# A softmax over 32768 columns: stores moved from GpSimd's queue to ScalarE's, loads pinned six tiles ahead

## The chip, the cores and the metric

One NeuronCore of a Trainium2 chip. The metric is the device time of one execution in microseconds (us), taken over several executions; a profile is taken of one such execution. On the profile's page an engine's busy share is the part of the span in which it works. A run is called slow when it is over 1.5% above the fastest run of the same kernel; ratios use the fast runs alone, while the times in us are medians of all runs. A ratio below is the mean time of one kernel's fast runs over that of the kernel before in the same rounds, on the same chip, so it is not quite the ratio of the medians quoted beside it.

## The reference

```python
def setup_inputs():
    batch, seq, vocab = 16, 256, 32768
    return {"logits": randn(batch, seq, vocab) as float32, "temperature": 1.0}

def reference(logits, temperature):
    scaled = logits / temperature
    scaled = scaled - scaled.max(axis=-1, keepdims=True)
    exp_scaled = np.exp(scaled)
    return exp_scaled / exp_scaled.sum(axis=-1, keepdims=True)
```

That is 537 MB in and 537 MB out, each touched once. Nothing is multiplied as a matrix; what matters is moving the bytes.

## The kernel before

Each row of 32768 columns is cut into four, so that a tile is 128 partitions x 8192 columns of float32 (4 MB), and there are 128 tiles. Six tile buffers fill the memory that is used on the core. A tile is worked in two chunks of 4096 columns. A tile has a first half (maxima on VectorE, exponentials with running sums on ScalarE, the minimum chain that joins the four quarter rows, and `ee`, a tiny exponential of 128x2) and a second half (the sum, its reciprocal, the factor `f`, two scalings, the store).

```python
for t in range(n_tiles):
    ...
    xs = xpool.tile([P, IC], fp32, tag="x", name="xs")          # one of six buffers
    nc.sync.dma_start(out=xs[:rp, :dn], in_=x[r0:r1, d0 : d0 + dn])
    for g0, gn in chop(dn, CC):                                 # two chunks
        nc.vector.tensor_reduce(out=nm[...], in_=xc, axis=X, op=A.max, negate=True)
        nc.scalar.activation(out=xc, in_=xc, func=Exp, bias=nm[...], accum_out=ssum[...])
    with tc.high_priority():
        nc.vector.tensor_reduce(out=nMh[...], in_=nm[:rp], axis=X, op=A.min)
        ...                                                     # shuffles and minima
        nc.scalar.activation(out=ee[:rp], in_=nm[:rp], func=Exp, bias=nM[:rp], scale=-1.0)
        nc.vector.tensor_tensor_reduce(out=ttj, in0=ee, in1=ssum, ...)   # the sum
        ...                                                     # shuffles, reciprocal
        nc.scalar.activation(out=f[:rp], in_=ee[:rp], func=Copy, scale=rS[:rp])
    ...
            nc.vector.tensor_scalar_mul(out=xc, in0=xc, scalar1=f[...])  # chunk 1
            nc.scalar.activation(out=xc, in_=xc, func=Copy, scale=f[...])  # chunk 0
    nc.gpsimd.dma_start(out=o[r0:r1, d0 : d0 + dn], in_=xs[:rp, :dn])
```

The source is not the issue order. A scheduler orders the instructions of each engine when the program is built, and the traces of this case show each engine working through its list in order: in the changed kernel ScalarE stands idle for 10.37 us before `ee` of tile 68 (1547.44 in the timeline further down), though the exponential that stands after it in the list (1547.82, the second chunk of tile 65) has had its maximum since 1471. So the built order has to be read from the built program or the trace.

Of the kernel before, what the change touches and what calls it, by code (L numbers as in the profile page):

```python
# [1 line left out]

# [4 lines left out]


_SPLIT = 4  # L10
_IC = 8192
_CC = 4096
_SBUF_KB = 192
_SCALE_ON_DVE = {1, 4, 7}


@with_exitstack
def kernel(
    ctx: ExitStack,
    tc: tile.TileContext,  # L20
    logits: bass.AP,
    temperature: bass.AP,
    out: bass.AP,
):
    nc = tc.nc

    inv_t = 1.0 / float(temperature)

    P = nc.NUM_PARTITIONS
    xf = logits.flatten_outer_dims()  # L30
    of = out.flatten_outer_dims()
    N, V = xf.shape

    SPLIT = _SPLIT
    while SPLIT > 1 and (V % SPLIT or (N * SPLIT) % P or V // SPLIT < 512):
        SPLIT //= 2
    x = xf.rearrange("n (h v) -> (n h) v", h=SPLIT) if SPLIT > 1 else xf
    o = of.rearrange("n (h v) -> (n h) v", h=SPLIT) if SPLIT > 1 else of
    NR, VR = x.shape
    n_tiles = (NR + P - 1) // P  # L40

    IC = min(_IC, VR)
    CC = min(_CC, IC)

    def chop(total: int, step: int) -> list[tuple[int, int]]:
        return [(s, min(step, total - s)) for s in range(0, total, step)]

    dchunks = chop(VR, IC)
    NDC = len(dchunks)
    NCH = len(chop(VR, CC))  # L50
    XBUFS = max(NDC + 2, (_SBUF_KB * 1024) // (IC * 4))

    xpool = ctx.enter_context(tc.tile_pool(name="x", bufs=XBUFS))
    spool = ctx.enter_context(tc.tile_pool(name="stats", bufs=8))

    fp32 = mybir.dt.float32
    Exp = mybir.ActivationFunctionType.Exp
    Copy = mybir.ActivationFunctionType.Copy
    X = mybir.AxisListType.X
    A = mybir.AluOpType  # L60
    n_rounds = SPLIT.bit_length() - 1

    for t in range(n_tiles):
        r0 = t * P
        r1 = min(r0 + P, NR)
        rp = r1 - r0

        nm = spool.tile([P, NCH], fp32, tag="nm", name="nm")
        ssum = spool.tile([P, NCH], fp32, tag="ssum", name="ssum")
        ee = spool.tile([P, NCH], fp32, tag="ee", name="ee")  # L70
        f = spool.tile([P, NCH], fp32, tag="f", name="f")
        ttj = spool.tile([P, NCH], fp32, tag="ttj", name="ttj")
        nMh = spool.tile([P, 1 + n_rounds], fp32, tag="nMh", name="nMh")
        Sh = spool.tile([P, 1 + n_rounds], fp32, tag="Sh", name="Sh")
        rS = spool.tile([P, 1], fp32, tag="rS", name="rS")

        slots = []
        c = 0
        for d0, dn in dchunks:
            xs = xpool.tile([P, IC], fp32, tag="x", name="xs")  # L80
            slots.append(xs)
            nc.sync.dma_start(out=xs[:rp, :dn], in_=x[r0:r1, d0 : d0 + dn])  # L82
            for g0, gn in chop(dn, CC):
                xc = xs[:rp, g0 : g0 + gn]
                nc.vector.tensor_reduce(  # L85
                    out=nm[:rp, c : c + 1], in_=xc, axis=X, op=A.max, negate=True
                )
                if inv_t != 1.0:
                    nc.vector.tensor_scalar_mul(
                        out=nm[:rp, c : c + 1], in0=nm[:rp, c : c + 1], scalar1=inv_t  # L90
                    )
                nc.scalar.activation(  # L92
                    out=xc,
                    in_=xc,
                    func=Exp,
                    bias=nm[:rp, c : c + 1],
                    scale=inv_t,
                    accum_out=ssum[:rp, c : c + 1],
                )
                c += 1  # L100

        with tc.high_priority():
            nc.vector.tensor_reduce(out=nMh[:rp, 0:1], in_=nm[:rp], axis=X, op=A.min)  # L103
            for j in range(n_rounds):
                mask = [i ^ (1 << j) for i in range(32)]
                nc.vector.stream_shuffle(  # L106
                    out=nMh[:rp, j + 1 : j + 2], in_=nMh[:rp, j : j + 1], mask=mask
                )
                nc.vector.tensor_tensor(  # L109
                    out=nMh[:rp, j + 1 : j + 2],  # L110
                    in0=nMh[:rp, j : j + 1],
                    in1=nMh[:rp, j + 1 : j + 2],
                    op=A.min,
                )
            nM = nMh[:, n_rounds : n_rounds + 1]
            nc.scalar.activation(  # L116
                out=ee[:rp], in_=nm[:rp], func=Exp, bias=nM[:rp], scale=-1.0
            )
            nc.vector.tensor_tensor_reduce(  # L119
                out=ttj[:rp],  # L120
                in0=ee[:rp],
                in1=ssum[:rp],
                scale=1.0,
                scalar=0.0,
                op0=A.mult,
                op1=A.add,
                accum_out=Sh[:rp, 0:1],
            )
            for j in range(n_rounds):
                mask = [i ^ (1 << j) for i in range(32)]  # L130
                nc.vector.stream_shuffle(  # L131
                    out=Sh[:rp, j + 1 : j + 2], in_=Sh[:rp, j : j + 1], mask=mask
                )
                nc.vector.tensor_tensor(  # L134
                    out=Sh[:rp, j + 1 : j + 2],
                    in0=Sh[:rp, j : j + 1],
                    in1=Sh[:rp, j + 1 : j + 2],
                    op=A.add,
                )
            nc.vector.reciprocal(out=rS[:rp], in_=Sh[:rp, n_rounds : n_rounds + 1])  # L140
            nc.scalar.activation(out=f[:rp], in_=ee[:rp], func=Copy, scale=rS[:rp])  # L141

        c = 0
        for i, (d0, dn) in enumerate(dchunks):
            xs = slots[i]
            for g0, gn in chop(dn, CC):
                xc = xs[:rp, g0 : g0 + gn]
                if (c % 8) in _SCALE_ON_DVE:
                    nc.vector.tensor_scalar_mul(  # L149
                        out=xc, in0=xc, scalar1=f[:rp, c : c + 1]  # L150
                    )
                else:
                    nc.scalar.activation(  # L153
                        out=xc, in_=xc, func=Copy, scale=f[:rp, c : c + 1]
                    )
                c += 1
            nc.gpsimd.dma_start(out=o[r0:r1, d0 : d0 + dn], in_=xs[:rp, :dn])  # L157


# [1 line left out]
_INS = ['logits', 'temperature']  # L161
_OUTS = [((16, 256, 32768), 'float32')]
#: Inputs that are plain numbers.
_NUMBERS = {'temperature': 1.0}


# [26 lines left out]
```

## Time and profile before

| | before |
|---|---|
| time, median of 4 runs | 2549.78 us (2544.84 to 2555.9) |
| span of the profiled run | 2541.2 us |
| DMA share, rate | 99.6% of 16 engines, 423 GB/s |
| VectorE, ScalarE busy | 61%, 59% |

From the page of the kernel before: the span, the busy times, the rows of 40 equal slices (each digit is the busy share in tenths, then GB/s), the DMA queues with packets, MB and share of the 16 engines, and the first line of the chain that ended last.

```profile
span 2541.2 us, 4377 instructions
...
DMA  9999999999999999999999999999999999999997
GB/s 413 431 430 429 424 428 429 426 427 425 424 427 424 429 424 422 424 427 422 423 425 419 429 424 426 424 425 426 423 428 424 426 425 427 426 424 423 425 426 327
...
q1 hardware_dynamic: 18432, 536.88, 50.6%
q0 software_dynamic: 18432, 536.88, 49.0%
...
DMA 87%; issue 6%; DVE 5%; another core or an unknown queue 0%; ACT 0%; POOL 0%; POOLq 0%; SPq 0%
```

The DMA row is at 9 in 39 of 40 slices, and loads (q1) and stores (q0) together take 99.6% of the engines. VectorE and ScalarE are idle for about two fifths of the time. In the trace's packet records the usual 32 KB packet takes 1213 ns on both queues; 32,768 such packets on 16 engines make 2484 us, which is the floor of the DMA work as measured here.

The longest waits of the kernel before, in total, in number, and the longest one:

```profile
POOL out_dram L157 <- DVE Sh L131: 2345.5, 122, 20.1
...
DVE nm L85 <- DMA xs<-in_logits_dram: 961.8, 125, 13.1
```

VectorE waits for data that DMA has not brought yet, and GpSimd's wait for VectorE is a store waiting for its tile: both go back to DMA. The queue that issues the loads (SPq, SyncE's) waits in turn for stores to land, once for each of the 122 loads after the first six, because a landed store is what frees a buffer:

```profile
SPq L82 <- DMA out_dram<-xs: 2400.7, 122, 61.0
```

The DMA issues, with the median time from issue to landing:

```profile
xs<-in_logits_dram SPq DMA_DIRECT2D x128, 4096.0 KB, 36.9
out_dram<-xs POOLq DMA_DIRECT2D x128, 4096.0 KB, 34.7
```

A transfer of 4 MB takes 37 us because about two loads and two stores share the engines (36.9 and 34.7 us at one of each per 19.8 us are 1.9 and 1.8 in flight). The first load, which is alone at the head of its queue, takes 12.3 us (issued at 0.74, landed at 13.08).

### The profile page before, as it was taken

The page shows a single profiled execution, that of the slowest core. Times are in us where ns is not written, and L with a number is a line of the kernel's source. Part 1 is how long each engine was busy: PE and PEld are TensorE (multiplying, and loading weights), DVE is VectorE, ACT ScalarE, POOL GpSimd, SP SyncE. Part 2 cuts the span into 40 slices and gives each one's busy share as a digit, 9 for nine tenths or more (in the row PEclk, how much of TensorE's full clock was granted, in tenths as well). Part 3 has the DMA queues.
Part 4 walks back from the last instruction along what each step waited for, and adds up shares of the span by engine and source line. Part 5 has one row for each costly group of instructions (what it writes and reads, how often), then busy time and mean ns, then how long its engine had stood idle before and what let it go on. Part 6 is the DMA issues. An engine that isn't in the chain of part 4 may idle for free.

```text
span 2541.2 us, 4377 instructions
## 1 busy us (share of the span) xinstructions
DVE 1548.3 (61%) x2432; ACT 1496.3 (59%) x897; POOL 70.2 (3%) x132
## 2 busy tenths in 40 slices
DVE  7665566665566655666556665666556665666554
ACT  6556655556656565565655566555665656555664
POOL 0000000000000000000000000000000000000000
DMA  9999999999999999999999999999999999999997
GB/s 413 431 430 429 424 428 429 426 427 425 424 427 424 429 424 422 424 427 422 423 425 419 429 424 426 424 425 426 423 428 424 426 425 427 426 424 423 425 426 327
DMA packets 36898, 1074.04 MB, mean 423 GB/s; under 512 B 4096, under 2 KB 4096, under 8 KB 4096
## 3 DMA queue, kind: packets, MB, share of 16 engines
q1 hardware_dynamic: 18432, 536.88, 50.6%
q0 software_dynamic: 18432, 536.88, 49.0%
q14 instruction: 34, 0.28, 0.0%
HBM read 536.87 MB, written 536.87 MB: 423 GB/s over the span
## 4 chain that ended last, share of the span: by engine, by line
DMA 87%; issue 6%; DVE 5%; another core or an unknown queue 0%; ACT 0%; POOL 0%; POOLq 0%; SPq 0%
DMA xs<-in_logits_dram 45%; DMA out_dram<-xs 43%; DVE xs L149 3%; DVE nm L85 2%; DVE ttj L119 0%; ACT xs L92 0%; POOL out_dram L157 0%; SPq L82 0%; POOLq L157 0%; DVE nMh L106 0%; DVE nMh L109 0%; DVE Sh L131 0%; POOLq L188 0%; DVE Sh L134 0%
## 5 line engine op out<-in xcount | busy, mean ns | idle before, releaser
L85 DVE TENSOR_REDUCE nm<-xs 128x1 f32<-128x4096 f32 x256 | 1130.1, 4415 | 961.8 <-DMA xs<-in_logits_dram 961.8
L92 ACT ACTIVATE xs<-xs,nm 128x4096 f32<-128x4096 f32 x256 | 949.2, 3708 | 1006.4 <-DVE nm L85 1006.4
L153 ACT ACTIVATE xs<-xs,f 128x4096 f32<-128x4096 f32 x128 | 474.5, 3707 | 4.2
L149 DVE TENSOR_SCALAR xs<-xs,f 128x4096 f32<-128x4096 f32 x128 | 300.7, 2350 | 0.8 <-ACT f L141 0.8
L157 POOL DMA_DIRECT2D out_dram<-xs x128 | 70.0, 547 | 2450.4 <-DVE Sh L131 2345.5
L92 ACT ACTIVATION_READ_ACCUMULATOR xs<-xs,nm 128x1 f32 x256 | 47.7, 186 | 0.0
L109 DVE TENSOR_TENSOR nMh<-nMh 128x1 f32<-128x1 f32 x256 | 40.9, 160 | 4.4
L134 DVE TENSOR_TENSOR Sh<-Sh 128x1 f32<-128x1 f32 x256 | 39.9, 156 | 0.0
L131 DVE STREAM_SHUFFLE Sh<-Sh 128x1 f32<-128x1 f32 x256 | 38.8, 152 | 0.0
L106 DVE STREAM_SHUFFLE nMh<-nMh 128x1 f32<-128x1 f32 x256 | 38.8, 152 | 0.0
L116 ACT ACTIVATE ee<-nm,nMh 128x2 f32<-128x2 f32 x128 | 35.8, 280 | 0.0
L141 ACT ACTIVATE f<-ee,rS 128x2 f32<-128x2 f32 x128 | 35.8, 280 | 0.0
L119 DVE CUSTOM_DVE_ANT_0 ttj<-ee,ssum 128x2 f32<-128x2 f32 x128 | 19.3, 151 | 3.1 <-ACT ee L116 3.1
L140 DVE RECIPROCAL rS<-Sh 128x1 f32<-128x1 f32 x128 | 21.0, 164 | 0.0
L103 DVE TENSOR_REDUCE nMh<-nm 128x1 f32<-128x2 f32 x128 | 19.8, 155 | 0.0
L119 DVE DVE_READ_ACCUMULATOR2_ANT Sh<- 128x1 f32 x128 | 10.6, 83 | 0.0
L92 ACT ACT_TABLE_LOAD x1 | 1.3, 1283 | 13.2 <-DMA xs<-in_logits_dram 13.2
L131 DVE LOAD_MASK_SELECT Sh<-Sh x256 | 3.6, 14 | 0.1
L106 DVE LOAD_MASK_SELECT nMh<-nMh x256 | 3.6, 14 | 0.1
L174 POOL MEMSET const-float32-0.0<- 128x1 f32 x1 | 0.1, 98 | 0.2 <-issue 0.2
L174 POOL MEMSET const-bfloat16-1.0<- 128x1 bf16 x1 | 0.1, 101 | 0.0
L174 POOL MEMSET const-float32-1.0<- 128x1 f32 x1 | 0.1, 98 | 0.0
(1 smaller groups left out, 0.1 us busy)
## 6 DMA issues: line engine op xcount, KB each, us to landing
xs<-in_logits_dram SPq DMA_DIRECT2D x128, 4096.0 KB, 36.9
out_dram<-xs POOLq DMA_DIRECT2D x128, 4096.0 KB, 34.7
```

What stands on the lines that cost most here:

```text
L85: nc.vector.tensor_reduce(out=nm[:rp, c : c + 1], in_=xc, axis=X, op=A.max, negate=True)
L92: nc.scalar.activation(out=xc, in_=xc, func=Exp, bias=nm[:rp, c : c + 1], scale=inv_t, accum_out=ssum[:rp, c : c + 1],)
L106: nc.vector.stream_shuffle(out=nMh[:rp, j + 1 : j + 2], in_=nMh[:rp, j : j + 1], mask=mask)
L109: nc.vector.tensor_tensor(out=nMh[:rp, j + 1 : j + 2], in0=nMh[:rp, j : j + 1], in1=nMh[:rp, j + 1 : j + 2], op=A.min,)
L116: nc.scalar.activation(out=ee[:rp], in_=nm[:rp], func=Exp, bias=nM[:rp], scale=-1.0)
L119: nc.vector.tensor_tensor_reduce(out=ttj[:rp], in0=ee[:rp], in1=ssum[:rp], scale=1.0, scalar=0.0, op0=A.mult, op1=A.add, accum_out=Sh[:rp, ...
L131: nc.vector.stream_shuffle(out=Sh[:rp, j + 1 : j + 2], in_=Sh[:rp, j : j + 1], mask=mask)
L134: nc.vector.tensor_tensor(out=Sh[:rp, j + 1 : j + 2], in0=Sh[:rp, j : j + 1], in1=Sh[:rp, j + 1 : j + 2], op=A.add,)
L141: nc.scalar.activation(out=f[:rp], in_=ee[:rp], func=Copy, scale=rS[:rp])
L149: nc.vector.tensor_scalar_mul(out=xc, in0=xc, scalar1=f[:rp, c : c + 1])
L153: nc.scalar.activation(out=xc, in_=xc, func=Copy, scale=f[:rp, c : c + 1])
L157: nc.gpsimd.dma_start(out=o[r0:r1, d0 : d0 + dn], in_=xs[:rp, :dn])
```

## The change

The intent: let the hardware queue of ScalarE issue the stores in place of GpSimd, keep the loads on SyncE in program order, and place six of them ahead. Besides, three of eight chunks are scaled by VectorE instead of four. The `high_priority` block stays. The core of the diff:

```diff
+    def load(t: int) -> None:
+        xs = xpool.tile([P, W], fp32, tag="x", name="xs")
+        slots[t] = xs
+        tc.keep_in_program_order(
+            nc.sync.dma_start(out=xs, in_=x[t * P : (t + 1) * P, :])
+        )
+    def store(t: int) -> None:
+        tc.keep_in_program_order(
+            nc.scalar.dma_start(out=o[t * P : (t + 1) * P, :], in_=slots.pop(t))
+        )
 ...
-                if (c % 8) in _SCALE_ON_DVE:
+            if (t * NCH + c) % 8 in _SCALE_ON_DVE:
 ...
-            nc.gpsimd.dma_start(out=o[r0:r1, d0 : d0 + dn], in_=xs[:rp, :dn])
+    for t in range(min(_AHEAD, n_tiles)):
+        load(t)
+    for t in range(n_tiles):
+        compute(t)
+        store(t)
+        if t + _AHEAD < n_tiles:
+            load(t + _AHEAD)
```

What the diff does not show is the order that comes out of the build. With the big work items only ("max 64" are the two maxima of tile 64, "exp 61.1" the exponential of its second chunk):

```
before   ScalarE: exp 62.0  exp 62.1  ee 62  f 61  scale 61.0 | exp 63.0  exp 63.1  ee 63  f 62 ...
         VectorE: max 62.0  sum 61  scale 60.1  max 62.1 | max 63.0  sum 62  scale 61.1 ...
changed  ScalarE: ee 64  f 60  exp 61.1  scale 60.0  f 61  STORE 60 | ee 65  scale 61.0  scale 61.1  exp 62.0  STORE 61 | ee 66 ...
         VectorE: max 64  sum 60  scale 60.1  sum 61 | max 65  max 66  sum 62  scale 62.0  sum 63  scale 63.1 | max 67 ...
```

`ee` of tile t+4 stands before the store of tile t, on the same engine, in order. The second half of a tile is now **four tiles behind** the loads.

More of the change, by code (lines that the diff above doesn't have):

```diff
@@ L7 @@
 from concourse._compat import with_exitstack
-_SPLIT = 4
-_IC = 8192
+_W = 8192
+_BUFS = 6
+_AHEAD = 6
 _CC = 4096
-_SBUF_KB = 192
 _SCALE_ON_DVE = {1, 4, 7}
@@ L29 @@
     P = nc.NUM_PARTITIONS
-    xf = logits.flatten_outer_dims()
-    of = out.flatten_outer_dims()
-    N, V = xf.shape
-    SPLIT = _SPLIT
-    while SPLIT > 1 and (V % SPLIT or (N * SPLIT) % P or V // SPLIT < 512):
-        SPLIT //= 2
-    x = xf.rearrange("n (h v) -> (n h) v", h=SPLIT) if SPLIT > 1 else xf
-    o = of.rearrange("n (h v) -> (n h) v", h=SPLIT) if SPLIT > 1 else of
-    NR, VR = x.shape
-    n_tiles = (NR + P - 1) // P
-    IC = min(_IC, VR)
-    CC = min(_CC, IC)
-    def chop(total: int, step: int) -> list[tuple[int, int]]:
-        return [(s, min(step, total - s)) for s in range(0, total, step)]
-    dchunks = chop(VR, IC)
-    NDC = len(dchunks)
-    NCH = len(chop(VR, CC))
-    XBUFS = max(NDC + 2, (_SBUF_KB * 1024) // (IC * 4))
-    xpool = ctx.enter_context(tc.tile_pool(name="x", bufs=XBUFS))
-    spool = ctx.enter_context(tc.tile_pool(name="stats", bufs=8))
     fp32 = mybir.dt.float32
@@ L60, with combine, compute @@
     A = mybir.AluOpType
-    n_rounds = SPLIT.bit_length() - 1
-    for t in range(n_tiles):
-        r0 = t * P
-        r1 = min(r0 + P, NR)
-        rp = r1 - r0
+    xf = logits.flatten_outer_dims()
+    of = out.flatten_outer_dims()
+    N, V = xf.shape
+    W = min(_W, V)
+    SPLIT = V // W
+    assert SPLIT * W == V and (N * SPLIT) % P == 0 and W % _CC == 0
+    x = xf.rearrange("n (h v) -> (n h) v", h=SPLIT)
+    o = of.rearrange("n (h v) -> (n h) v", h=SPLIT)
+    n_tiles = N * SPLIT // P
+    n_rounds = SPLIT.bit_length() - 1
+    NCH = W // _CC
+    xpool = ctx.enter_context(tc.tile_pool(name="x", bufs=_BUFS))
+    spool = ctx.enter_context(tc.tile_pool(name="stats", bufs=8))
+    slots = {}
+    def load(t: int) -> None:
[8 more added lines that the diff above has]
+        )
+    def combine(v, op) -> None:
+        for j in range(n_rounds):
+            mask = [i ^ (1 << j) for i in range(32)]
+            nc.vector.stream_shuffle(
+                out=v[:, j + 1 : j + 2], in_=v[:, j : j + 1], mask=mask
+            )
+            nc.vector.tensor_tensor(
+                out=v[:, j + 1 : j + 2],
+                in0=v[:, j : j + 1],
+                in1=v[:, j + 1 : j + 2],
+                op=op,
+            )
+    def compute(t: int) -> None:
+        xs = slots[t]
         nm = spool.tile([P, NCH], fp32, tag="nm", name="nm")
@@ L75 @@
         rS = spool.tile([P, 1], fp32, tag="rS", name="rS")
-        slots = []
-        c = 0
-        for d0, dn in dchunks:
-            xs = xpool.tile([P, IC], fp32, tag="x", name="xs")
-            slots.append(xs)
-            nc.sync.dma_start(out=xs[:rp, :dn], in_=x[r0:r1, d0 : d0 + dn])
-            for g0, gn in chop(dn, CC):
-                xc = xs[:rp, g0 : g0 + gn]
-                nc.vector.tensor_reduce(
-                    out=nm[:rp, c : c + 1], in_=xc, axis=X, op=A.max, negate=True
-                )
-                if inv_t != 1.0:
-                    nc.vector.tensor_scalar_mul(
-                        out=nm[:rp, c : c + 1], in0=nm[:rp, c : c + 1], scalar1=inv_t
-                    )
-                nc.scalar.activation(
-                    out=xc,
-                    in_=xc,
-                    func=Exp,
-                    bias=nm[:rp, c : c + 1],
-                    scale=inv_t,
-                    accum_out=ssum[:rp, c : c + 1],
-                )
-                c += 1
@@ L102 @@
-        with tc.high_priority():
-            nc.vector.tensor_reduce(out=nMh[:rp, 0:1], in_=nm[:rp], axis=X, op=A.min)
-            for j in range(n_rounds):
-                mask = [i ^ (1 << j) for i in range(32)]
-                nc.vector.stream_shuffle(
-                    out=nMh[:rp, j + 1 : j + 2], in_=nMh[:rp, j : j + 1], mask=mask
-                )
-                nc.vector.tensor_tensor(
-                    out=nMh[:rp, j + 1 : j + 2],
-                    in0=nMh[:rp, j : j + 1],
-                    in1=nMh[:rp, j + 1 : j + 2],
-                    op=A.min,
-                )
-            nM = nMh[:, n_rounds : n_rounds + 1]
-            nc.scalar.activation(
-                out=ee[:rp], in_=nm[:rp], func=Exp, bias=nM[:rp], scale=-1.0
+        for c in range(NCH):
+            xc = xs[:, c * _CC : (c + 1) * _CC]
+            nc.vector.tensor_reduce(
+                out=nm[:, c : c + 1], in_=xc, axis=X, op=A.max, negate=True
+            )
+            if inv_t != 1.0:
+                nc.vector.tensor_scalar_mul(
+                    out=nm[:, c : c + 1], in0=nm[:, c : c + 1], scalar1=inv_t
+                )
+            nc.scalar.activation(
+                out=xc,
+                in_=xc,
+                func=Exp,
+                bias=nm[:, c : c + 1],
+                scale=inv_t,
+                accum_out=ssum[:, c : c + 1],
+            )
@@ L118 @@
+        with tc.high_priority():
+            nc.vector.tensor_reduce(out=nMh[:, 0:1], in_=nm, axis=X, op=A.min)
+            combine(nMh, A.min)
+            nc.scalar.activation(
+                out=ee,
+                in_=nm,
+                func=Exp,
+                bias=nMh[:, n_rounds : n_rounds + 1],
+                scale=-1.0,
             )
             nc.vector.tensor_tensor_reduce(
-                out=ttj[:rp],
-                in0=ee[:rp],
-                in1=ssum[:rp],
+                out=ttj,
+                in0=ee,
+                in1=ssum,
@@ L126 @@
                 op1=A.add,
-                accum_out=Sh[:rp, 0:1],
+                accum_out=Sh[:, 0:1],
             )
-            for j in range(n_rounds):
-                mask = [i ^ (1 << j) for i in range(32)]
-                nc.vector.stream_shuffle(
-                    out=Sh[:rp, j + 1 : j + 2], in_=Sh[:rp, j : j + 1], mask=mask
-                )
-                nc.vector.tensor_tensor(
-                    out=Sh[:rp, j + 1 : j + 2],
-                    in0=Sh[:rp, j : j + 1],
-                    in1=Sh[:rp, j + 1 : j + 2],
-                    op=A.add,
-                )
-            nc.vector.reciprocal(out=rS[:rp], in_=Sh[:rp, n_rounds : n_rounds + 1])
-            nc.scalar.activation(out=f[:rp], in_=ee[:rp], func=Copy, scale=rS[:rp])
-        c = 0
-        for i, (d0, dn) in enumerate(dchunks):
-            xs = slots[i]
-            for g0, gn in chop(dn, CC):
-                xc = xs[:rp, g0 : g0 + gn]
-                if (c % 8) in _SCALE_ON_DVE:
-                    nc.vector.tensor_scalar_mul(
-                        out=xc, in0=xc, scalar1=f[:rp, c : c + 1]
-                    )
-                else:
-                    nc.scalar.activation(
-                        out=xc, in_=xc, func=Copy, scale=f[:rp, c : c + 1]
-                    )
-                c += 1
-            nc.gpsimd.dma_start(out=o[r0:r1, d0 : d0 + dn], in_=xs[:rp, :dn])
+            combine(Sh, A.add)
+            nc.vector.reciprocal(out=rS, in_=Sh[:, n_rounds : n_rounds + 1])
+            nc.scalar.activation(out=f, in_=ee, func=Copy, scale=rS)
+        for c in range(NCH):
+            xc = xs[:, c * _CC : (c + 1) * _CC]
+            if (t * NCH + c) % 8 in _SCALE_ON_DVE:
+                nc.vector.tensor_scalar_mul(out=xc, in0=xc, scalar1=f[:, c : c + 1])
+            else:
+                nc.scalar.activation(out=xc, in_=xc, func=Copy, scale=f[:, c : c + 1])
+    for t in range(min(_AHEAD, n_tiles)):
[5 more added lines that the diff above has]
+            load(t + _AHEAD)
 _INS = ['logits', 'temperature']
```

## The prediction

> **What bounds the kernel now.** DMA. The page's DMA row reads 9 (90% or more) in 39 of 40 slices, 423 GB/s over the span; the queues take 50.6 + 49.0 = 99.6% of the 16 engines. DVE is busy 61%, ACT 59%. In the packet records the usual 32 KB packet takes 1213 ns on either queue; 32,768 of them on 16 engines make 2484 us, so of the 2541 us span at most some 57 us (2.2%) can be won by DMA alone. About 42 us of that are load packets that take longer (mean 1254 ns; store packets 1215), bunched just after each GpSimd issue.
>
> **What the change does.**
> 1. The stores' issue leaves GpSimd (128 x 0.55 us, off the path). The Trainium skill, "DMA: Bandwidth & Descriptors", section "Issuing engines are not separate DMA queues", says all of them run on the same 16 DMA engines; the equal 1213 ns agree. Possible gain: part of those 42 us.
> 2. Of eight 128x4096 scalings in 4 tiles, 3 are on DVE and 5 on ACT instead of 4 and 4; both engines have slack.
> 3. What decides: the issue order. Before, DVE runs tile t's sum right after the first maximum of t+1, so a store needs one later load. In the changed kernel's issue order, ACT runs the small exponential ee of tile t+4 before the scaling and store of tile t, and DVE takes sum t after the maxima of t+4. So store t waits for load t+4, and load t+6 waits for store t's landing (six buffers). Only two independent chains, even and odd tiles, are left, each: load lands, compute, store, load.
>
> **Cost of a chain (estimate from the durations of before).** A lone 4 MB transfer takes 12.3 us from issue to landing (first load: 0.74 to 13.08), then 0.14 us to the next issue; a store and a load: 24.8 us. Compute from landing of t+4 to issue of store t: two maxima 8.75, minimum chain and ee 1.4, then the ACT work that stands before the store: about 8 us (exp, scale) or 12 us (two exp, scale), so 18.2 and 22.0 us on even tiles. Four tiles: 2 x 24.8 + 18.2 + 22.0 = 89.8 us, and about 1.7 us for sharing with the odd chain: 91.5 us, where DMA work is 8 x 9.71 = 78 us. Before: 4 x 19.85 = 79.4 us. The odd chain has a similar sum and is held about half a cycle behind by the DVE order (maxima of t+5 only after t's and t+1's sums). The start is about 30 us later (fifth store near 138 us, before 107.5), 29 cycles make 2654, the drain about 125 us: span 2917 us, reported time some 10 us more.
>
> **Prediction: 2925 us, 8 in 10 within 2760 to 3030. Faster by over 2%: 3%; within 2%: 5%; slower by over 2%: 92%.**
>
> **What would show it.** DMA row at 8 with gaps instead of 9; about 370 GB/s; ACT waiting long on DVE at the line of ee, and DVE waiting on loads at the maxima; time from issue to landing down from 36.9 and 34.7 us to 12 to 20, since transfers rarely share; store issues at uneven distances, 91 us per four. Load packets near 1213 ns would show that the GpSimd issues had slowed them.
>
> **What would make it wrong.** If the chains overlap better (less compute after the landing than I count), DMA stays full and the time is 2500 to 2545. If the two chains fall into step, so that their transfers collide and then both compute, 96 to 105 us per four tiles: above 3030.

## More of the kernel before

The timeline of the kernel before, around the store of tile 60 (start, duration, engine, line, operation). The maximum at 1214.00 is the first of tile 62:

```profile
1214.00 4.42 DVE L85 TENSOR_REDUCE nm<-xs 128x1 f32<-128x4096 f32 x1 [8.52 <-DMA xs<-in_logits_dram]
...
1218.33 0.15 DVE L119 CUSTOM_DVE_ANT_0 ttj<-ee,ssum 128x2 f32<-128x2 f32 x1
...
1218.41 2.35 DVE L149 TENSOR_SCALAR xs<-xs,f 128x4096 f32<-128x4096 f32 x1
...
1220.75 4.41 DVE L85 TENSOR_REDUCE nm<-xs 128x1 f32<-128x4096 f32 x1
1221.31 0.53 POOL L157 DMA_DIRECT2D out_dram<-xs  x1 [20.12 <-DVE Sh L131]
```

VectorE scales tile 60 (1218.41) only after the first maximum of tile 62. So the store of tile 60 (1221.31) waits for the load of tile 62: the second half of a tile stands **two tiles behind** the loads.

## The result, and the profile after

| | before | changed |
|---|---|---|
| time, median of 4 runs | 2549.78 us | 2997.28 us (2994.88 to 2998.55) |
| ratio of fast runs | | 1.1748 (95% interval 1.1723 to 1.1773) |
| span of the profiled run | 2541.2 us | 2996.8 us |
| DMA share, rate | 99.6%, 423 GB/s | 87.6%, 358 GB/s |
| VectorE, ScalarE busy | 61%, 59% | 51%, 53% |

The changed kernel is 17.5% slower. Its page, the same lines as before:

```profile
span 2996.8 us, 4063 instructions
...
DMA  9998888889888898888888888888888888888886
GB/s 417 387 371 350 364 353 347 364 350 364 355 359 357 357 364 350 350 357 358 355 363 358 356 352 357 363 358 357 357 362 366 357 357 357 359 362 357 354 367 287
...
q1 hardware_dynamic: 18432, 536.88, 45.9%
q10 hardware_dynamic: 18432, 536.88, 41.7%
...
DMA 51%; DVE 27%; ACT 16%; issue 5%; another core or an unknown queue 0%; SPq 0%; ACTq 0%
```

The DMA row has fallen mostly to 8 from the fourth slice on, and the chain that ended last is now a mix: DMA 51%, VectorE 27%, ScalarE 16%. No engine is full. That is the picture of a dependency cycle, not of a busy resource. Its longest waits:

```profile
ACT ee L106 <- DVE nMh L67: 1374.5, 126, 19.0
DVE nm L87 <- DMA xs<-in_logits_dram: 1093.7, 93, 18.6
```

The first line is new: ScalarE stands for 1374 us, 126 times, at `ee`, waiting for VectorE's minimum chain of a tile four ahead, which itself waits for that tile's load (second line). Before, ScalarE never waited at `ee`. The loads wait for stores to land as before, so a late store makes a late load:

```profile
SPq L53 <- DMA out_dram<-xs: 2833.5, 122, 51.8
```

The DMA issues:

```profile
xs<-in_logits_dram SPq DMA_DIRECT2D x128, 4096.0 KB, 14.5
out_dram<-xs ACTq DMA_DIRECT2D x128, 4096.0 KB, 12.8
```

Transfers land in 13 to 15 us instead of 35 to 37: they are hardly ever queued behind another of their own kind (7 of 128 loads and 3 of 128 stores were issued while one was in flight). A transfer that gets faster while the kernel gets slower is a sign that the queues run empty. One turn of the cycle in the timeline of the changed kernel; the maxima at 1537.69 are tile 68's, the store at 1555.24 is tile 64's, the load at 1566.46 is tile 70's, into the buffer that tile 64 has left, and the maxima at 1582.13 are tile 70's:

```profile
1537.69 8.74 DVE L87 TENSOR_REDUCE nm<-xs 128x1 f32<-128x4096 f32 x2 [15.63 <-DMA xs<-in_logits_dram]
...
1547.44 0.29 ACT L106 ACTIVATE ee<-nm,nMh 128x2 f32<-128x2 f32 x1 [10.37 <-DVE nMh L67]
1547.64 0.28 ACT L125 ACTIVATE f<-ee,rS 128x2 f32<-128x2 f32 x1
1547.82 3.69 ACT L94 ACTIVATE xs<-xs,nm 128x4096 f32<-128x4096 f32 x1
...
1551.52 3.69 ACT L132 ACTIVATE xs<-xs,f 128x4096 f32<-128x4096 f32 x1
...
1555.24 0.34 ACTq L58 DMA_DIRECT2D out_dram<-xs  x1
...
1566.46 0.33 SPq L53 DMA_DIRECT2D xs<-in_logits_dram  x1
...
1582.13 4.42 DVE L87 TENSOR_REDUCE nm<-xs 128x1 f32<-128x4096 f32 x1 [16.25 <-DMA xs<-in_logits_dram]
```

Read it as a ring. Load 68 lands; maxima; at 1547.44 `ee` of tile 68 at last lets ScalarE go on to `f`, the exponential and the scaling that stand before store 64 (17.55 us from the first maximum to the store). Store 64 lands 11.22 us later and at once frees the buffer for load 70. Load 70 lands 15.67 us later, which releases store 66. Even tiles form one such ring, odd tiles another; with six buffers and a distance of four there are just 6 - 4 = 2. Averaged over the run, the even ring takes per four tiles 17.55 + 21.24 us of compute, 11.32 + 11.27 us of stores and 16.85 + 15.66 us of loads: 93.9 us, and stores are 93.9 us apart per four tiles. In the kernel before four tiles took 79.3 us.

### The profile page after: what moved, and what is told of

Its sections match the earlier page's. It is cut to its first block, busy times and chain, and to the rows that moved or that the text cites. A ratio compares the mean times of both kernels' runs of the same rounds, so it can differ in the third digit from the quotient of the medians.

```text
span 2996.8 us, 4063 instructions
## 1 busy us (share of the span) xinstructions
DVE 1538.0 (51%) x2400; ACT 1584.4 (53%) x929; POOL 0.2 (0%) x4
## 4 chain that ended last, share of the span: by engine, by line
DMA 51%; DVE 27%; ACT 16%; issue 5%; another core or an unknown queue 0%; SPq 0%; ACTq 0%
DMA xs<-in_logits_dram 33%; DVE nm L87 23%; DMA out_dram<-xs 18%; ACT xs L94 12%; ACT xs L132 3%; DVE xs L130 1%; ACT f L125 1%; DVE nMh L64 1%; DVE nMh L67 1%; ACT ee L106 1%; DVE nMh L104 0%; DVE Sh L64 0%; DVE Sh L67 0%; DVE ttj L113 0%
## 5 line engine op out<-in xcount | busy, mean ns | idle before, releaser
L132 ACT ACTIVATE xs<-xs,f 128x4096 f32<-128x4096 f32 x160 | 587.8, 3693 | 0.5 <-ACT f L125 0.5
L130 DVE TENSOR_SCALAR xs<-xs,f 128x4096 f32<-128x4096 f32 x96 | 225.9, 2353 | 197.5 <-ACT f L125 197.5
L104 DVE TENSOR_REDUCE nMh<-nm 128x1 f32<-128x2 f32 x128 | 19.8, 155 | 3.2
## 6 DMA issues: line engine op xcount, KB each, us to landing
xs<-in_logits_dram SPq DMA_DIRECT2D x128, 4096.0 KB, 14.5
out_dram<-xs ACTq DMA_DIRECT2D x128, 4096.0 KB, 12.8
```

Of the source, the lines that this page charges most:

```text
L104: nc.vector.tensor_reduce(out=nMh[:, 0:1], in_=nm, axis=X, op=A.min)
L130: nc.vector.tensor_scalar_mul(out=xc, in0=xc, scalar1=f[:, c : c + 1])
L132: nc.scalar.activation(out=xc, in_=xc, func=Copy, scale=f[:, c : c + 1])
```

## The experiments

Each kernel gives the reference's result. First the two single edits, then a family with everything pinned. In that family every instruction is kept in program order, and the program order is: first half of tile t, then second half and store of tile t - `_LATE`, then the next load.

```python
for t in range(n_tiles + _LATE):
    if t < n_tiles:
        first(t)                       # maxima, exponentials, minimum chain, ee
    if t >= _LATE:
        second(t - _LATE)              # sum, f, one scaling on each engine
        store(t - _LATE)               # ScalarE or GpSimd
        if t - _LATE + _AHEAD < n_tiles:
            load(t - _LATE + _AHEAD)
```

| run | what it is | distance | buffers | stores from | time, us | ratio to before |
|---|---|---|---|---|---|---|
| e1 | before, one word changed | 4 | 6 | ScalarE | 2930.0 | 1.157 |
| e2 | changed, one word back | 1 to 2 | 6 | GpSimd | 2578.6 | see below |
| e8 | pinned | 0 | 6 | ScalarE | 2499.3 | 0.985 |
| e10 | pinned | 0 | 6 | GpSimd | 2500.1 | 0.985 |
| e11 | pinned | 0 | 4 | ScalarE | 2507.8 | 0.988 |
| e3 | pinned | 1 | 6 | ScalarE | 2563.9 | 1.012 |
| e4 | pinned | 1 | 6 | GpSimd | 2550.1 | 1.005 |
| e7 | pinned | 3 | 6 | ScalarE | 2604.6 | 1.026 |
| e5 | pinned | 4 | 6 | ScalarE | 2911.6 | 1.150 |
| e6 | pinned | 4 | 6 | GpSimd | 2946.0 | 1.162 |
| e9 | pinned | 5 | 6 | ScalarE | 5039.6 | 1.984 |
| e12 | pinned, half-width tiles | 4 | 12 | ScalarE | 2548.1 | 1.006 |

(Medians of all runs. The kernel before had medians of 2541.5, 2547.7 and 2542.2 us beside these, with runs from 2512.6 to 2563.0. e1 to e4 ran on one chip, e5 to e8 on a second and e9 to e12 on a third, so across these groups compare the ratios.)

The theory: the loss is the issue order, which puts a store four tiles behind the loads. Rival A: it is another part of the change, such as the pinned loads. Rival B: it is the hardware queue on ScalarE, slow in itself or in ScalarE's way.

### e1: the kernel before, stores from ScalarE

```diff
-            nc.gpsimd.dma_start(out=o[r0:r1, d0 : d0 + dn], in_=xs[:rp, :dn])
+            nc.scalar.dma_start(out=o[r0:r1, d0 : d0 + dn], in_=xs[:rp, :dn])
```

> The kernel before with one word changed: its stores are issued by ScalarE. In the built program this one word also changes the issue order: ScalarE runs ee of tile t+4 before the store of tile t, and VectorE sums tile t after the maxima of tile t+4 (before: t+1). Order theory: slow like the changed kernel, 2900 to 3000 us. Rival A (the loads' program order, the 3:5 split of scalings or the way loads are placed six ahead cost the time): 2500 to 2560 us. Rival B (a store issued by ScalarE's hardware queue is itself slow or holds up ScalarE) also expects slow, so this run tells only A from the rest.

Measured: 2930.0 us, ratio 1.157 (1.149 to 1.165). One word makes nearly the whole loss; the pinned loads, the number of loads ahead and the share of scalings are not needed for it. Rival A falls. The waits show the same new line as the changed kernel's: ScalarE at `ee`, 1421 us in 126 waits. The word does two things at once, though: it moves the stores to another queue and it makes the scheduler order both compute engines anew. The changed kernel is a further 1.5% slower than e1 by the ratios; its part from maxima to store is longer (means over the middle third 17.4 us against 15.7), but which piece of the change makes that was not tested.

### e2: the changed kernel, stores from GpSimd

```diff
-            nc.scalar.dma_start(out=o[t * P : (t + 1) * P, :], in_=slots.pop(t))
+            nc.gpsimd.dma_start(out=o[t * P : (t + 1) * P, :], in_=slots.pop(t))
```

> The changed kernel with its stores issued by GpSimd again. The built program then has tile t summed after the first maximum of t+1, mostly, and nothing of t+4 ahead of a store. Order theory and rival B (hardware queue slow): 2530 to 2570 us. Rival A: stays near 2990 us.

Measured: four runs, 2522.1, 2571.8, 2585.3 and 2589.6 us. Three are counted as slow (more than 1.5% above the first), so there is no ratio, and the median of 2578.6 is 9 us above what was expected. Against 2997 us the answer is plain all the same: the rest of the change stays in, and the loss is gone. What is left is order or queue.

### e3 and e4: distance 1 pinned, both queues

> Every instruction pinned to program order; the second half (sum, scaling, store) of tile t follows the first half (maxima, exponentials, ee) of tile t+1, as before; stores from ScalarE. Order theory: DMA stays full, at most 2550 us; near 2510 us if the GpSimd issues slowed load packets (mean load packet near 1215 ns instead of 1254), near 2550 us if not. Rival B (the queue itself is slow): near 2990 us.

> The same pinned program, stores from GpSimd. Both theories: 2540 to 2560 us with load packets of a mean near 1254 ns, slow ones bunched after GpSimd issues. The difference to the ScalarE twin is what the queue alone is worth: 35 to 40 us if GpSimd issues slow load packets, none if they don't.

("As before" is wrong in the first text: the kernel before has a distance of two. No pinned run has that distance.) Measured: 2563.9 us with ScalarE's queue (ratio 1.012, 1.005 to 1.018) and 2550.1 us with GpSimd's (1.005, 0.998 to 1.012). The first is a small miss: at most 2550 us was expected. Rival B falls all the same: with the order held, the two queues are 0.7% apart by these ratios, with intervals that overlap, not 17%. The hoped-for gain fails too. In e3, without a single GpSimd issue, load packets had a mean of 1270 ns, longer than in the kernel before (1254); in e4 it was 1248. So load packets can be slow without any GpSimd issue.

### e5 and e6: distance 4 pinned, both queues

```diff
-_LATE = 1
+_LATE = 4
```

> The pinned program of e3 with one number changed: the second half of tile t follows the first half of tile t+4 instead of t+1. Store t then waits for load t+4, load t+6 for store t: a cycle of one lone store (12.3 us), one lone load (12.3 us), 0.2 us of issue and about 17 us of compute between (two maxima 8.8, an exponential 3.8, ee and f 0.5, a scaling 3.7), shared by 6 - 4 = 2 tiles: about 21 to 22 us per tile. Order theory: 2780 us, 2700 to 2850. Rival (the order does not matter, something else of the change or of e1 costs the time): 2560 us as e3.

> The same with stores from GpSimd. Order theory: as e5 within 1% (GpSimd's longer issue adds a few tenths of a us to each cycle), so the queue has no part in it. Rival B (hardware queue on ScalarE is needed for the loss): 2550 us as e4.

From e5's page:

```profile
span 2911.7 us, 4254 instructions
...
DMA  8999999888999998989998899998989989999898
```

Measured: 2911.6 us (ratio 1.150) and 2946.0 us (1.162). One number in the order brings the loss back, with either queue: this is the experiment that settles it. But both lie above the range of 2700 to 2850, and the two differ by 1.2% where 1% was allowed. The ring shows why the first is so: from store to the next load's issue 14.6 us, from there to the maxima 14.1, compute 16.7, together 45.4 us for two tiles, where I had 42 to 44. Compute came out as expected; the transfers did not. I had counted lone transfers, with at most 2 us for sharing. In e5's trace 122 of 128 stores are issued while a load, the other ring's, is still in flight, so a store shares the DMA engines at its start and a load at its end. In e6 the compute part is 0.3 us longer (17.0) and the store part 0.5 us (15.1); why was not tested.

### e7: distance 3

> Three tiles between the halves: the same cycle of about 42 us is shared by 3 tiles, 14 us per tile, less than the 19.4 us that the DMA engines need. Order theory: back at the DMA bound, 2520 to 2580 us; the loss has a threshold and is not proportional to the distance. A theory of a cost per tile of distance (more waits, more latency) would put it two thirds of the way to e5.

Measured: 2604.6 us, ratio 1.026 (1.016 to 1.037), a little above the range. Of the 348 us between e3 and e5, the first two steps of distance cost 41 and the third 307. The loss has a threshold, as the ring says: lone transfers and compute (about 40 us) shared by three tiles are less than the 19.4 us per tile that DMA needs, shared by two they are just more. (The lone times alone would make 20 us per tile at distance 4; the 22.7 us of e5 come from the sharing as well.) But e7 is not quite free: its rate is only 414 GB/s, with packets longer on both queues (1257 and 1244 ns), while its DMA row is full:

```profile
DMA  9999999999999999999999999999999999999998
```

### e8: distance 0

> No distance: every tile is finished before the next is begun. Order theory: DMA bound, as e3 within 1%, perhaps 5 to 10 us less from an earlier first store and a shorter drain. If VectorE's and ScalarE's waits for each other inside a tile (about 5 us per tile) mattered, it would be slower; they have slack, about 12 us of busy time and 5 of waits in 19.8 us.

Measured: 2499.3 us in all of six runs (2499.2 to 2499.5), ratio 0.985 (0.981 to 0.990). That is 2.5% under e3, more than expected. From its page: the span, the DMA row and the DMA issues.

```profile
span 2497.7 us, 4377 instructions
...
DMA  9999999999999999999999999999999999999997
...
xs<-in_logits_dram SPq DMA_DIRECT2D x128, 4096.0 KB, 53.1
out_dram<-xs ACTq DMA_DIRECT2D x128, 4096.0 KB, 44.7
```

By its page it moved 430 GB/s over the span, and the span is 14 us above the packet floor of 2484. Transfers now stand 53 and 45 us from issue to landing: nothing waits in a buffer for a second half, so all the slack lies in the DMA queues. Load packets have a mean of 1214.6 ns. VectorE waits 395 us in total for `ee` inside a tile, while DMA stays full.

### e9: distance 5

> Five tiles between the halves: one tile left to share the cycle, so store and load are each alone on the DMA engines. Cycle: 12.3 + 12.3 us of transfer, 0.2 us of issue, 16.8 us from landing to store (as measured in e5: 1507.35 to 1524.08): 41.6 us per tile, about 120 of them, and a start and a drain of some 150 us. Order theory: 5000 to 5350 us. A theory of a fixed cost per tile of distance: e5 is about 350 us over e3 for three tiles, so some 3030 us.

Measured: 5039.6 us, inside the range. This is the purest form of the ring: one tile at a time, nothing shared. Its timeline, the maxima of a tile, `ee`, the store of the tile five before, the load that takes its buffer, and that load's maxima:

```profile
2510.48 8.75 DVE L92 TENSOR_REDUCE nm<-xs 128x1 f32<-128x4096 f32 x2 [24.85 <-DMA xs<-in_logits_dram]
...
2522.97 0.28 ACT L109 ACTIVATE ee<-nm,nMh 128x2 f32<-128x2 f32 x1
...
2527.21 0.34 ACTq L60 DMA_DIRECT2D out_dram<-xs  x1
2538.43 0.33 SPq L56 DMA_DIRECT2D xs<-in_logits_dram  x1
2550.57 4.42 DVE L92 TENSOR_REDUCE nm<-xs 128x1 f32<-128x4096 f32 x1 [24.75 <-DMA xs<-in_logits_dram]
```

16.73 us from the maxima to the store, 11.22 to the landing and next issue, 12.14 to the next maxima: 40.1 us, and stores are 40.15 us apart over the run. A theory in which each tile of distance costs a fixed time expected some 3030 us and falls.

### e10: distance 0, stores from GpSimd

> e8 with stores from GpSimd, which says what part of e8's 1.5% gain over the kernel before is the ScalarE queue's. If the gain is of the order alone: 2499 to 2510 us and load packets of a mean near 1215 ns in spite of 128 GpSimd issues. If GpSimd issues slow load packets (my blind prediction's reading): 2535 to 2545 us, as before.

Measured: 2500.05 us, ratio 0.985 (0.981 to 0.989); load packets 1214.6 ns, as in e8. So the gain is not the queue's; it goes with the order. The change of queue, which the change was meant to be about, makes 0.8 us between these two medians (taken on two chips) and nothing in the ratios. The Trainium skill, "DMA: Bandwidth & Descriptors", section "Issuing engines are not separate DMA queues", says just that: issuing engines share the same DMA engines and only issue time is saved. e8 against e10 agrees.

### e11: distance 0 with four buffers

```diff
-_BUFS = 6
-_AHEAD = 6
+_BUFS = 4
+_AHEAD = 4
```

> e8 with four buffers and four tiles ahead instead of six. DMA bound either way (a cycle of 24.8 + 18 us shared by 4 tiles is 11 us per tile). Slack theory (e8 is faster because finishing a tile at once leaves more time in which a buffer's transfer stands in a DMA queue, 53 + 45 us in e8 against 37 + 35 in the kernel before, so that no DMA engine runs dry when one engine falls behind): with two buffers less these sum to about 60 us, less than before, so slow load packets come back and it takes 2530 to 2610 us. If it is the order of work as such: 2499 to 2505 us.

Measured: 2507.8 us (2506.5 to 2508.9), ratio 0.988; issue to landing 26.5 and 32.7 us, which sum to 59 as expected, but load packets of 1223 ns only. It lies 3 us above the range for the order and 22 us below that for slack. The slack theory in the form that I stated falls: with less slack than the kernel before it is still 1.2% faster than it. For the main question it agrees with the ring: two buffers fewer cost 0.3% when the distance is zero (e10, on the same chip, took 2500.05 us).

### e12: distance 4 with twelve buffers of half the size

> e5 (four tiles between the halves) with tiles of half the width and twelve buffers instead of six, the same bytes of SBUF. The cycle is now shared by 12 - 4 = 8 tiles of 2 MB and is about 8 + 8 us of transfer and 13 us of compute, under 4 us per tile where DMA needs 9.7. Order theory: DMA bound again, 2500 to 2600 us; the loss is in buffers minus distance, not in the order by itself. If the early issue of ee and the late sums were bad in themselves: near e5, 2900 us.

Measured: 2548.1 us, ratio 1.006 (0.9995 to 1.012). The same distance in tiles as e5, the same bytes of buffers, and the loss is gone, as 12 - 4 = 8 rings that share the cycle would have it. The early `ee` and late sum are not bad in themselves. What e12 does not separate: its four tiles are half as wide, so in bytes the distance is halved too, as with six full-width tiles at a distance of two. That the number of buffers counts, and not the bytes of distance alone, rests on the traces, in which 122 loads wait for a store to land (before and changed); no run changed the number of full-width buffers at a distance above zero.

### One sum for all runs

Time per tile = (store issue to next load's issue + load issue to maxima + compute from there to the store) / (buffers - distance). It holds in every run because it is the ring itself; what it tells is which side gives way. Means over the middle of each run, in us:

| run | store | load | compute | shared by | sum / shared | DMA |
|---|---|---|---|---|---|---|
| before | 35.0 | 36.9 | 7.3 | 4 | 19.8 | full |
| e10 | 47.4 | 51.1 | 18.4 | 6 | 19.5 | full |
| e11 | 33.1 | 26.8 | 18.1 | 4 | 19.5 | full |
| e7 | 21.5 | 22.2 | 16.7 | 3 | 20.2 | full |
| e5 | 14.6 | 14.1 | 16.7 | 2 | 22.7 | gaps |
| e9 | 11.2 | 12.2 | 16.7 | 1 | 40.1 | half empty |

Where DMA is full, transfers stretch in their queues until the sum fits the 19.5 to 20.2 us per tile that DMA takes there. When they are down to what a lone transfer needs (11.2 and 12.2 us in e9), they cannot shrink further, and the kernel waits. The changed kernel is at 23.5 us per tile with 2 shared.

### What stays open

Why the kernel before and the runs with distance 1 have slow load packets, and so lose 1.5 to 2.5% to e8, was not settled. Two explanations fell (GpSimd issues in e3 and e10, little slack in e11). Slow load packets do follow the issue of a store, but from either engine: those that start within 5 us of it have a mean of 1284 ns in the kernel before (GpSimd) and 1338 in e3 (ScalarE), those of the next 5 us 1239 and 1224. One more observation is left. The rate of e2 in 40 slices:

```profile
GB/s 414 433 433 432 433 432 433 432 433 432 434 433 433 434 432 433 434 433 433 432 432 433 433 432 433 433 433 435 433 426 431 416 409 419 422 406 421 421 414 324
```

e2 ran at 433 GB/s for three quarters of its span and then dropped. In its records the time between the first and the last of a transfer's 16 engines to finish grew steadily, from 2.7 us at 200 to 400 us to 12.6 at 1600 to 1800, and 18.4 at 2000 to 2200. From about the time of the drop, in about half of the loads 10 to 13 engines had finished the previous load when the next was issued, and the mean load packet went from 1214 to about 1300 ns. So in this run slow load packets came together with engines that had run out of loads. In the kernel before and in e4, however, load packets are slow before the engines drift that far apart. No experiment was made on it, so this is an observation, not a cause.

## Why the prediction was right, point by point

- **"of the 2541 us span at most some 57 us (2.2%) can be won by DMA alone"** Right: e8 reaches a span of 2497.7 us, and nothing went under the packet floor of 2484.
- **"What decides: the issue order."** Right in the mechanism, with the two chains that it named (the rings above). e1 and e2 show that the issuing word makes it, e3 to e6 that the order does it and not the queue; e7, e9 and e12 agree that buffers minus distance is the number that counts. The aside **"so a store needs one later load"** on the kernel before was misread: it needs two. The argument did not rest on it.
- **"Four tiles: 2 x 24.8 + 18.2 + 22.0 = 89.8 us, and about 1.7 us for sharing with the odd chain: 91.5 us"** Measured 93.9. The compute terms were 17.55 and 21.24 us against 18.2 and 22.0 predicted; a store with the next issue 11.3 against 12.4; the loads 32.5 us per four tiles against 24.8 + 1.7 for sharing. So the term that was mis-sized is the sharing of the DMA engines between the two chains: about 6 us too small on the loads, set off in part by stores and compute that were 3.6 us too large. Over 29 cycles the difference of 2.4 us makes 70 of the 80 us by which the span of 2917 was too low. That the total came so near is in part luck, as errors of +6 and -3.6 us met.
- **"The start is about 30 us later (fifth store near 138 us, before 107.5), 29 cycles make 2654, the drain about 125 us"** Measured 141.0 us for the fifth store, and 130.5 us from the store of tile 120 to the end.
- **"DMA row at 8 with gaps instead of 9; about 370 GB/s; ACT waiting long on DVE at the line of ee"**, with transfers of 12 to 20 us: right. 358 GB/s, 8 with some 9s, 1374 us at `ee`, medians of 14.5 and 12.8 us. The reason given there, **"since transfers rarely share"**, was too strong: 92 of 128 stores were issued while a load was in flight, and that is the sharing that was mis-sized.
- **"Load packets near 1213 ns would show that the GpSimd issues had slowed them."** Wrong as a sign and as an idea. In the changed kernel the mean was 1342 ns, mainly because the first 16 packets of a load had a mean of about 1.86 us (loads 10 to 124); and e3 and e10 show that GpSimd issues are not what slows loads.
- **"A lone 4 MB transfer takes 12.3 us from issue to landing"**: e9 has 11.2 us for a store and 12.2 for a load, the next issue or the wake of VectorE included. The Trainium skill, "DMA: Bandwidth & Descriptors", section "Anatomy of one DMA — SWDGE (gpsimd) path", gives a fit of 2.0 us plus bytes over 436 GB/s for DMAs from GpSimd; an estimate from it for 4,194,304 bytes is 11.6 us. These transfers are from the hardware queues and lie on either side of it.

## What to carry to other kernels

With B buffers and a second half that stands D tiles behind the loads, load t+B waits for store t, and store t for load t+D, so that B - D tiles share one turn of a ring; when the lone latencies of one turn (store, load, the compute between) divided by B - D exceed the busiest engine's time per tile, the kernel falls off that engine, abruptly (here between three tiles sharing and two), and by more than the quotient says where the rings' transfers collide. So read the built order before anything else, because changing the engine that issues a DMA can make a scheduler reorder everything around it, and pin the order if it matters: finishing each tile before beginning the next was both the simplest order and the fastest here, at 2499.3 us. Long queues with short compute are good news (53 us from issue to landing in the fastest kernel), and short transfer times beside idle DMA engines are bad news (13 us in the slow one).

## What the Trainium skill lacked or had wrong

- "DMA: Bandwidth & Descriptors", section "Issuing engine by pattern", names SyncE for simple loads and stores and calls the sync and scalar path "generally faster" than GpSimd's. At 4 MB per transfer the runs show it only at distance 4, where DMA has gaps: 2911.6 us with stores from ScalarE and 2946.0 from GpSimd. With DMA full it was 2499.3 and 2500.05 at distance 0, 2563.9 and 2550.1 at distance 1.
- The same page, section "Latency and other measured facts", ties DMA engines that lag to GpSimd's descriptor ring, as a best guess. With no GpSimd DMA at all (e8), the spread between the first and the last engine of a transfer still grew, from 2.6 us at 200 to 400 us to 14.1 us at 2200 to 2400. Which engines lag, the records do not say.
- "Perfetto Trace Analysis", section "Optimization Strategy", names missing buffers as a reason for repeating gaps. It does not say that the issue order uses buffers up: with the same six, pinned distances of 0, 3, 4 and 5 took 2499.3, 2604.6, 2911.6 and 5039.6 us.
- No page says that the choice of the issuing engine can change the order in which a scheduler lays out the compute engines: one word in e1 moved the distance from two to four and the time from 2541.5 to 2930.0 us.
